# A two-layer DiT block on one core: maxima over partitions by a TensorE product in the FFN and the w_out stage

## The chip, the core and the metric

The kernel runs on one core of a Trainium2 chip. Its time is the device time of one execution in microseconds. Three runs of the kernel before took 3187.04, 3192.05 and 3198.25 us, median 3192.05. One more execution was profiled; it took 3185.58 us.

## The reference

Two layers over 1024 tokens (`x`) and 256 context tokens (`ctx`), width 1024. The context is carried only through layer 0. Everything is float32.

```python
for l in range(2):
    mod, mod_c = silu(c) @ w_ada[l] + b_ada[l], silu(c_ctx) @ w_ada[l] + b_ada[l]   # shifts, scales, gates
    h = modulate(layer_norm(x), sh1, sc1)              # the same for ctx
    qa, ka, va, qb, kb, vb, zh, zf = split(h @ w_in[l])
    oa = banded_window_attention(rope(qa), rope(ka), va, ctx keys and values, sink)
    ob = blockwise_full_attention(rope(rms(qb)), rope(rms(kb)), vb, ctx keys and values)
    oc = hyena_mixer(zh); od = fnet_mixer(zf)          # long convolution, Fourier mixing
    y = rms_per_group(oa, ob, oc, od) * g @ w_out[l] + b_out[l]
    x = layer_norm(4 ** 0.25 * x + g1 * y)
    h2 = modulate(layer_norm(x), sh2, sc2)
    a, g = split(dwconv3(h2 @ w_up + b_up))            # 2 x 2752 columns, convolution over tokens
    x = layer_norm(4 ** 0.25 * x + g2 * ((silu(a) * g) @ w_down + b_down))
```

## The kernel before

**Products in pairs of float16.** Nearly every float32 operand of a product is scaled by a power of two and split into two float16 parts, `hi` and `lo`; a product is then three matmuls (hi*hi, hi*lo, lo*hi). The power of two (`pow2`, L79) comes from a bound on the whole operand, so the kernel often needs the largest absolute value of a tile over its free dimension and over its 128 partitions. VectorE's reduction gives the first. The second is `allmax` (L89): for each column of its input two copies of 64 partitions, a maximum, four copies of 32 partitions, a maximum broadcast to 32 columns, a 32x32 block transpose and a reduction, ten VectorE instructions, in the tiles `arc` and `arb` of a pool with one buffer.

**Weights.** `load_w` (L375) fetches a weight tile of float32 into `wraw` (four buffers, 512 KB each, shared by all weight loads and the residuals), reduces it on VectorE, calls `most` (L109) and so `allmax`, and splits it with ScalarE (hi) and VectorE (lo) into `w16` tiles (four buffers). w_in and w_out are bounded by the root of a sum of squares instead (`root`, L119), which calls `allmax` too. `load_wd` (L1263) does the same for up to three 128-row tiles of w_down at once.

**Stages of a layer.** `project` (products with w_in, beside hyena and FNet work), `attend`, `out_proj` (w_out, residual, two normalizations, the FFN's input `h2` in float16 pairs) and `ffn`. In `out_proj` three up tiles are loaded ahead (`UA`, L985 to L987).

**The FFN** (L1027). The 5504 up columns are 43 tiles of 128: one tile of 64 + 64 columns (`w_upl`, column 42), worked first as a group of its own, and 21 pairs (gate half and value half) in seven groups of three. `up` (L1058) takes a weight tile that was loaded ahead or loads it, multiplies it with all tokens (48 matmuls of 512 columns, in layer 0 another 24 of 256 for the context) into the PSUM tile `ux` (two buffers in layer 0, three in layer 1), and applies bias and convolution on ScalarE (L1077) and VectorE (L1078, L1080) with a correction of the two edge tokens on GpSimd. A pair is multiplied after SiLU and reduced to its maximum (L1168). At the end of a group `load_wd` brings w_down's rows, `allmax` turns the group's maxima into one scale (`gm`, `gsp`), `gh` and `gl` are split, and `down` and `add` multiply them with w_down into `dps` (PSUM, two buffers) and add to `acc` on VectorE (L1112). The first half of the tokens is added right away, the second half after the next group's scale, so that these matmuls lie beside that chain.

**The last group** has the residual and the gate worked into `acc` beside it (`residual`, L1119), and its sums go tile by tile through the final normalization (`first`, `second`); in layer 0 a third `dps` buffer comes in here (`fdx`, L1144), and `third` builds the next layer's input. In layer 0 the FFN also carries layer 1's hyena filter (`filter_ahead`, L1323), whose PSUM tile `fps` has a pool of one bank.

**Order of the work.** The code is traced in program order; a planner then orders each engine's instructions before the run, by readiness in its own time model and by program order among what is ready. On the chip each engine follows the written order and waits on semaphores. Buffers of one tile name are handed out by the planner as earlier ones come free.

Of the kernel before, what the change touches and what calls it, by code (L numbers as in the profile page):

```python
# [59 lines left out]
class Kernel:  # L60
# [28 lines left out]
    def allmax(self, out, in_):  # L89


        v = self.nc.vector
        for i in range(in_.shape[1]):
            x = in_[:, i:i + 1]
            c = self.ar.tile([128, 4], FT, name="arc")
            for h in (0, 64):
                v.tensor_copy(c[h:h + 64, 0:1], x[64 - h:128 - h])
            v.tensor_tensor(c[:, 1:2], x, c[:, 0:1], op=OP.max)
            for q in range(0, 128, 32):
                v.tensor_copy(c[q:q + 32, 2:3], c[q ^ 32:(q ^ 32) + 32, 1:2])  # L100
            b = self.ar.tile([128, 2, 32], FT, name="arb")
            v.tensor_tensor(b[:, 0], c[:, 1:2].to_broadcast([128, 32]), c[:, 2:3].to_broadcast([128, 32]), op=OP.max)
            v.transpose(b[:, 1], b[:, 0])
            v.tensor_reduce(out[:, i:i + 1], b[:, 1], axis=AX.X, op=OP.max)
# [38 lines left out]
    def consts(self):  # L143
# [5 lines left out]
        nc.vector.tensor_copy(self.identh, self.identf)  # L149
        self.mhalf = p.tile([128, 8], FT, name="mhalf")  # L150
# [15 lines left out]
    def tables(self):  # L166
# [9 lines left out]
        nc.vector.tensor_scalar(self.mask, mk, -(2.0 ** 50), None, op0=OP.mult)  # L176
        self.bigi = p.tile([128, 128], BF, name="bigi")
        nc.vector.tensor_scalar(self.bigi, self.identf, 2.0 ** 50, None, op0=OP.mult)
# [157 lines left out]
    def start(self):  # L336
# [3 lines left out]
        self.bgp = self.pool("bgp", self.p2, bufs=3, space=PSUM, side=self.sides[1])  # L340
        with ExitStack() as es:
# [66 lines left out]
    def run(self, out):  # L408
        for l in range(2):
            self.l = l  # L410
            self.p2 = ExitStack()
            if l == 0:
                self.start()
            else:
                self.bgp = self.pool("bgp", self.p2, bufs=3, space=PSUM, side=self.sides[1])
            self.project(l)
# [262 lines left out]
    def attend(self, l):  # L679
        nc = self.nc  # L680
        A, B = self.sides
        with ExitStack() as es:
            tp = self.pool("atm", es, bufs=2, side=A)
            pt = self.pool("atp", es, space=PSUM, side=A)
            po = self.pool("ato", es, space=PSUM, side=B)
            nt = NT if l == 0 else NX
# [18 lines left out]
    def att_main(self, l, tp, pt, pq):  # L705
# [29 lines left out]
        def top(ch, h):  # L735
# [9 lines left out]
            for t in range(nq):  # L745
# [7 lines left out]
                for i, (k0, k1) in enumerate(parts):  # L753
# [6 lines left out]
                    for b, m in masks:  # L760
                        nc.tensor.matmul(ps[:, (b - k0) * 128:(b - k0 + 1) * 128], self.bigi, self.mask[:, m],
# [33 lines left out]
        def scores(ch, h, b0, i, k, q0, q1):  # L795
# [12 lines left out]
            for b, m in masks:  # L808
                nc.tensor.matmul(ps[:, (b - b0) * 128:(b - b0 + 1) * 128], self.bigi, self.mask[:, m],
                                 start=False, stop=True, skip_group_check=True)  # L810
# [148 lines left out]
    def out_proj(self, l):  # L959
# [6 lines left out]
        with ExitStack() as es:  # L966
# [6 lines left out]
            pp = self.pool("oph", es, bufs=2, space=PSUM, side=B)  # L973
            lg, lb = self.row_bcast(cp, a["ln1_g"][l], "rlg"), self.row_bcast(cp, a["ln1_b"][l], "rlb")
# [52 lines left out]
    def ffn(self, l, out):  # L1027
# [6 lines left out]
        with ExitStack() as es:  # L1034
# [10 lines left out]
            dp = self.pool("fdp", es, bufs=2, space=PSUM, side=B)  # L1045
            eup = es.enter_context(ExitStack())
# [11 lines left out]
            def up(col, src, pool, early=False):  # L1058

                whi, wlo, winv = self.upw.pop(0) if self.upw else self.load_w(src, 128, None, sp, "up")  # L1060
# [3 lines left out]
                parts = [(pp.tile([128, 1024], FT, name="ux", bufs=2 + l), 0, L)]  # L1064
# [71 lines left out]
            if l == 0:  # L1136
                self.bg = [self.filter_ahead(1, self.pool("fha", eha, side=B), self.pool("fpp", eha, space=PSUM, side=B))]
            for gi, grp in enumerate(groups):
                if gi == len(groups) - 1:
# [3 lines left out]
                    if l == 0:  # L1143
                        dpr.append(self.pool("fdx", es, bufs=1, space=PSUM, side=B))  # L1144
# [6 lines left out]
                for i, j in enumerate(grp):  # L1151
                    k = 128
                    if j < 21:
                        g32 = up(2 * j, a["w_up"][l, j, :, :, 0:128], g3)
                        if gi == len(groups) - 1:
                            self.tick(RT[0])
                        ug = up(2 * j + 1, a["w_up"][l, j, :, :, 128:256], tp)
                        nc.scalar.activation(g32, g32, AF.Silu)
                        nc.vector.tensor_mul(g32, g32, ug)
                    else:  # L1160
                        k = 64
                        g32 = up(42, a["w_upl"][l], g3, True)
# [780 lines left out]
```

## Time and profile before

| | |
|---|---|
| profiled execution | 3185.58 us |
| its span, first to last instruction | 3183.8 us |
| TensorE matmuls (PE) | 2849.6 us busy, 90% |
| TensorE weight loads (PEld) | 1510.6 us, 47% |
| VectorE (DVE) | 2474.5 us, 78% |
| ScalarE (ACT) | 1315.0 us, 41% |
| GpSimd (POOL) | 864.4 us, 27% |
| mean granted TensorE clock | 0.946 of full speed |
| chain that ended last | TensorE 52%, VectorE 32% of the span |

In the profile the FFN of layer 0 runs from about 860 to 1740 us and that of layer 1 from about 2420 us to the end; `out_proj` lies ahead of each. An instruction's row gives its line in the kernel, its engine, operation, output and input tiles. A value in brackets, with an arrow, is time that the engine stood idle just before, and the instruction that ended the wait. In a row of a group of instructions, the figures after the bar are busy time, mean length of one in ns, and idle time before them with what ended most of it. A matmul's length holds its passage through the array; in a stream they start closer together than they are long.

### The profile page before, as it was taken

The numbers are of one execution on the slowest core, as the hardware profiler recorded it, in microseconds if no ns is written. First come the engines' busy times: TensorE is split into PE (matmuls) and PEld (weight loads), VectorE is DVE, ScalarE is ACT, GpSimd is POOL, SyncE is SP. The second block draws the span as 40 slices with busy tenths as digits, with TensorE's granted clock in tenths as the row PEclk, the third lists the DMA queues.
The fourth block names the chain that finished last, engine by engine and source line by source line (L and its number), as shares of the span: only waits on it lengthen the run. The fifth ranks groups of instructions, "written<-read, shape, count | busy, mean of one in ns | idle before, by whom it ended". The sixth has DMA issues, their size and how long they took to land.

```text
span 3183.8 us, 46231 instructions
## 1 busy us (share of the span) xinstructions
PE 2849.6 (90%) x17268; PEld 1510.6 (47%) x17268; DVE 2474.5 (78%) x5678; ACT 1315.0 (41%) x2098; POOL 864.4 (27%) x886
## 2 busy tenths in 40 slices
PE   5998878899999999999999799967898799999997
PEld 1567744345444554544544356734554244444443
DVE  4989578865788677677588789789976878777788
ACT  3566555554543222222223765665655222222222
POOL 1337335643500000000020736446633000000022
PEclk8999979999999999999999899967999899999998
DMA  7253465561311121121120344442022122111121
GB/s 260 84 174 105 137 208 186 174 206 67 125 44 55 37 67 50 34 67 50 34 94 33 119 146 128 145 130 61 22 79 76 53 60 60 37 50 40 54 86 53
DMA packets 214926, 293.76 MB, mean 92 GB/s; under 512 B 36189, under 2 KB 156425, under 8 KB 213549
## 3 DMA queue, kind: packets, MB, share of 16 engines
q1 hardware_dynamic: 205629, 269.57, 26.4%
q0 software_dynamic: 9072, 21.24, 2.5%
q8 instruction: 135, 2.21, 0.3%
q14 instruction: 90, 0.74, 0.1%
HBM read 240.05 MB, written 50.71 MB: 91 GB/s over the span
## 4 chain that ended last, share of the span: by engine, by line
PE 52%; DVE 32%; DMA 5%; ACT 4%; issue 4%; POOL 3%; SPq 0%; DVEq 0%; POOLq 0%; ACTq 0%
PE ux L1073 24%; PE uc L1073 3%; DVE M L763 2%; DVE acc L1112 2%; PE ada L216 2%; PE dps L1092 2%; PE zps L562 2%; PE zps L563 2%; PE zps L561 2%; DVE ph L816 2%; PE dps L1094 2%; PE dps L1095 2%; DVE arc L100 2%; DVE gl L140 2%; DMA wraw<-in_w_up 1%
## 5 line engine op out<-in xcount | busy, mean ns | idle before, releaser
L1073 PE MATMUL ux<-h2h,w 128*128 128x512 f16 x2752 | 836.0, 381 | 11.2 <-ACT w L139 4.8
L1073 PEld LDWEIGHTS <-w 128*128 128x128 f16 x5160 | 503.6, 98 | 523.4 <-issue 13.1
L1073 PE MATMUL ux<-h2l,w 128*128 128x512 f16 x1376 | 523.6, 381 | 0.6 <-POOL h2l L325 0.6
L1083 POOL TENSOR_TENSOR u<-u,ed 128x2 f32<-128x2 f32 x129 | 34.0, 263 | 1331.9 <-DVE u L1080 1208.5
L1092 PE MATMUL dps<-wdh,gh 128*128 128x512 f16 x792 | 307.7, 389 | 71.1 <-DVE acc L1112 24.3
L817 POOL TENSOR_TENSOR pl<-p,ph 128x512 f16<-128x512 f32 (+1 forms) x224 | 239.5, 1084 | 195.6 <-DVE ph L816 115.0
L1094 PE MATMUL dps<-wdl,gh 128*128 128x512 f16 x756 | 291.4, 385 | 0.0
L1095 PE MATMUL dps<-wdh,gl 128*128 128x512 f16 x756 | 289.8, 384 | 0.0
L1078 DVE SCALAR_TENSOR_TENSOR u<-ux,ws,u 128x1023 f32<-128x1023 f32 x86 | 109.7, 1278 | 228.9 <-ACT u L1077 228.8
L1077 ACT ACTIVATE u<-ux,cb,ws 128x1024 f32<-128x1024 f32 x86 | 103.2, 1202 | 415.5 <-PE ux L1073 415.0
L812 ACT ACTIVATE p<-sps,al 128x512 f32<-128x512 f32 (+3 forms) x288 | 169.7, 618 | 121.9 <-PE sps L806 41.5
L763 DVE TENSOR_REDUCE M<-mps 128x1 f32<-128x512 f32 (+2 forms) x336 | 173.3, 535 | 31.9 <-PE mps L758 18.5
L139 ACT ACTIVATE w<-wraw,upp 128x1024 f16<-128x1024 f32 x80 | 91.6, 1144 | 223.0 <-DVE upp L86 223.0
L758 PE MATMUL mps<-kT,qT 128*128 128x512 f16 (+2 forms) x336 | 116.7, 365 | 61.9 <-DVE M L763 58.4
L561 PE MATMUL zps<-w,hh 128*128 128x256 f16 x608 | 168.1, 276 | 2.4 <-ACT zt L608 2.4
L563 PE MATMUL zps<-w,hl 128*128 128x256 f16 x608 | 168.5, 277 | 0.0
L562 PE MATMUL zps<-w,hh 128*128 128x256 f16 x608 | 168.5, 277 | 0.0
L1112 DVE SCALAR_TENSOR_TENSOR acc<-dps,gm,acc 128x512 f32<-128x512 f32 x198 | 146.6, 743 | 6.7 <-PE dps L1095 5.5
L1092 PEld LDWEIGHTS <-gh 128*128 128x128 f16 x792 | 78.4, 99 | 133.1 <-DVE gh L140 21.8
L139 ACT ACTIVATE gh<-u,gsp 128x640 f16<-128x640 f32 (+3 forms) x88 | 61.5, 764 | 190.9 <-DVE gsp L86 175.2
L1094 PEld LDWEIGHTS <-gh 128*128 128x128 f16 x756 | 74.8, 99 | 130.3 <-issue 52.0
L816 DVE CAST ph<-p 128x512 f16<-128x512 f32 (+3 forms) x200 | 115.3, 587 | 26.8 <-ACT p L812 25.6
(562 smaller groups left out, 6878.2 us busy)
## 6 DMA issues: line engine op xcount, KB each, us to landing
wraw<-in_w_ada SPq DMA_DIRECT2D x96, 512.0 KB
wraw<-in_w_up SPq DMA_DIRECT2D x84, 512.0 KB
wraw<-in_w_down SPq DMA_DIRECT2D x42, 512.0 KB
wraw<-in_w_in SPq DMA_DIRECT2D x32, 512.0 KB
wraw<-xd SPq DMA_DIRECT2D x26, 512.0 KB
xd<-rx SPq DMA_DIRECT2D x18, 512.0 KB
wraw<-in_w_out SPq DMA_DIRECT2D x16, 512.0 KB
M<-in_k_mf POOLq DMA_DIRECT2D x24, 256.0 KB, 3.6
```

Of the source, the lines that this page charges most:

```text
L561: nc.tensor.matmul(ps, ah[:, kt], bh[:, kt], start=kt == ks[0], stop=False)
L562: nc.tensor.matmul(ps, ah[:, kt], bl[:, kt], start=False, stop=False)
L563: nc.tensor.matmul(ps, al[:, kt], bh[:, kt], start=False, stop=kt == ks[-1])
L763: nc.vector.tensor_reduce(M[:, t, i:i + 1], ps[:, :n], axis=AX.X, op=OP.max)
L812: nc.scalar.activation(p32, ps[:, c], AF.Exp, scale=self.al[ch][:, 0:1])
L816: nc.vector.tensor_copy(ph[:, c], p32)
L817: (nc.vector if i % 4 == 2 else nc.gpsimd).tensor_tensor(pl[:, c], p32, ph[:, c], op=OP.subtract)
L1073: nc.tensor.matmul(o, w[:, kt], h[:, kt, t0:t0 + n], start=first, stop=last)
L1092: nc.tensor.matmul(ps, gh[:, i, c], w[0][:, i, hc], start=f, stop=False)
L1094: nc.tensor.matmul(ps, gh[:, i, c], w[1][:, i, hc], start=False, stop=False)
L1095: nc.tensor.matmul(ps, gl[:, i, c], w[0][:, i, hc], start=False, stop=e)
L1112: nc.vector.scalar_tensor_tensor(acc[t][:, hc], ps, sc, bt[:, hc] if gi == 0 else acc[t][:, hc], op0=OP.mult, op1=OP.add)
```

## The change

`allmax` gets a second form, used where `self.mx` gives a PSUM tile: for each column the upper 16 bits of the float32 maxima (a bfloat16 with the same exponent) are the stationary operand, broadcast to 128 columns, and the identity is the moving operand. Each of the 128 output partitions then holds all 128 maxima, and one VectorE reduction gives the largest. `self.mx` is set in `out_proj` and `ffn`; at the start, in `project` and in `attend` the ten copies stay, under the name `allmax_copies`.

For its PSUM tile `out_proj` opens a bank of its own (`opm`). In `ffn` the pool `fpp` serves both the maxima and the filter's tiles, in both layers; `ux` has two buffers in layer 1 as well, and the third `dps` buffer of layer 0's last group goes.

`up` no longer loads its own tile. At each call, if fewer than three tiles are waiting, the next of the list is loaded; then the oldest is taken, so that a load stands two tiles ahead of its use in program order. In attention the mask's factor 2^100 sits in the mask alone, and the identity in bfloat16 takes the place of `bigi`.

```diff
     def allmax(self, out, in_):
+        if self.mx is None:
+            return self.allmax_copies(out, in_)
+        nc = self.nc
+        n = in_.shape[1]
+        ps = self.mx()[:, :n * 128].rearrange("p (n q) -> p n q", n=n)
+        for c in range(n):
+            m = in_[:, c:c + 1].bitcast(BF)[:, 1:2]
+            nc.tensor.matmul(ps[:, c], m.to_broadcast([128, 128]), self.identb, start=True, stop=True)
+        nc.vector.tensor_reduce(out, ps, axis=AX.X, op=OP.max)
+
+    def allmax_copies(self, out, in_):
...
+        self.identb = p.tile([128, 128], BF, name="identb")
+        nc.vector.tensor_copy(self.identb, self.identf)
...
-        nc.vector.tensor_scalar(self.mask, mk, -(2.0 ** 50), None, op0=OP.mult)
-        self.bigi = p.tile([128, 128], BF, name="bigi")
-        nc.vector.tensor_scalar(self.bigi, self.identf, 2.0 ** 50, None, op0=OP.mult)
+        nc.vector.tensor_scalar(self.mask, mk, -(2.0 ** 100), None, op0=OP.mult)
...
             pp = self.pool("oph", es, bufs=2, space=PSUM, side=B)
+            mp = self.pool("opm", es, bufs=1, space=PSUM, side=B)
+            self.mx = lambda: mp.tile([128, 512], FT, name="mx")
...
             dp = self.pool("fdp", es, bufs=2, space=PSUM, side=B)
+            mp = self.pool("fpp", es, space=PSUM, side=B)
+            self.mx = lambda: mp.tile([128, 512], FT, name="fps")
...
-            def up(col, src, pool, early=False):
-                whi, wlo, winv = self.upw.pop(0) if self.upw else self.load_w(src, 128, None, sp, "up")
+            srcs = [a["w_upl"][l]] + [a["w_up"][l, j, :, :, i * 128:(i + 1) * 128] for j in range(21) for i in range(2)]
+            srcs = srcs[len(self.upw):]
+            def up(col, pool, early=False):
+                if srcs and len(self.upw) < 3:
+                    self.upw.append(self.load_w(srcs.pop(0), 128, None, sp, "up"))
+                whi, wlo, winv = self.upw.pop(0)
...
-                parts = [(pp.tile([128, 1024], FT, name="ux", bufs=2 + l), 0, L)]
+                parts = [(pp.tile([128, 1024], FT, name="ux", bufs=2), 0, L)]
...
-                self.bg = [self.filter_ahead(1, self.pool("fha", eha, side=B), self.pool("fpp", eha, space=PSUM, side=B))]
+                self.bg = [self.filter_ahead(1, self.pool("fha", eha, side=B), mp)]
...
-                    if l == 0:
-                        dpr.append(self.pool("fdx", es, bufs=1, space=PSUM, side=B))
```

## Rows read from the trace of the kernel before

**Rows 1.** Windows: length; busy (count) of PE, PEld, DVE, ACT, POOL; clock; DMA; GB/s.

```profile
860.00:1000.00 140.00, 124.97 (x608) 58.98 (x606) 116.04 (x278) 59.49 (x77) 13.01 (x27) 0.91 0.16 48
1000.00:1600.00 600.00, 589.31 (x3054) 299.14 (x3053) 427.80 (x979) 140.81 (x147) 23.90 (x63) 1.00 0.16 49
1600.00:1800.00 200.00, 173.17 (x834) 83.66 (x833) 164.97 (x399) 77.14 (x101) 65.89 (x65) 0.94 0.24 80
2420.00:2580.00 160.00, 122.86 (x532) 52.49 (x531) 125.11 (x323) 50.98 (x56) 13.65 (x20) 0.88 0.18 54
2580.00:3000.00 420.00, 414.06 (x1908) 186.06 (x1906) 321.69 (x747) 106.18 (x105) 8.92 (x28) 1.00 0.17 52
3000.00:3184.00 184.00, 154.65 (x702) 68.71 (x700) 153.11 (x302) 48.48 (x55) 46.38 (x36) 0.94 0.17 60
2540.00:2560.00 20.00, 12.49 (x47) 4.86 (x47) 18.88 (x78) 5.97 (x8) 0.00 (x0) 0.72 0.17 52
```

**Rows 2.** TensorE's timeline, layer 1's entry: start, length, instruction [idle before, releaser].

```profile
2481.67 0.61 PE L1092 MATMUL dps<-wdh,gh 128*128 128x512 f16 x1 [20.80 <-DVE gh L140]
2547.12 0.61 PE L1092 MATMUL dps<-wdh,gh 128*128 128x512 f16 x1 [6.32 <-ACT gh L139]
```

**Rows 3.** VectorE's timeline over the same stretch.

```profile
2423.66 2.33 DVE L395 TENSOR_REDUCE upmx<-wraw 128x1 f32<-128x1024 f32 x2
2474.00 0.31 DVE L97 COPY arc<-gm 64x1 f32<-64x1 f32 x2
2477.92 0.31 DVE L97 COPY arc<-upmx 64x1 f32<-64x1 f32 x2
```

**Rows 4.** Copies' groups: busy us, mean ns, idle before.

```profile
L97 DVE COPY arc<-upmx 64x1 f32<-64x1 f32 x160 | 23.7, 148 | 3.7
L98 DVE TENSOR_TENSOR arc<-upmx,arc 128x1 f32<-128x1 f32 x80 | 13.5, 169 | 0.0
L100 DVE COPY arc<-arc 32x1 f32<-32x1 f32 x600 | 87.0, 145 | 11.7
L102 DVE TENSOR_TENSOR arb<-arc 128x32 f32<-128x32 f32 x150 | 34.0, 227 | 1.1
L103 DVE STREAM_TRANSPOSE arb<-arb 128x32 f32<-128x32 f32 x150 | 30.8, 205 | 1.7
L104 DVE TENSOR_REDUCE upmo<-arb 128x1 f32<-128x32 f32 x80 | 14.5, 181 | 1.0
```

**Rows 5.** Groups by shape: score reductions, mask product, up weight loads.

```profile
L763 DVE TENSOR_REDUCE M<-mps 128x1 f32<-128x256 f32 x160 | 65.4, 415 | 11.4 <-PE mps L758 10.5 <-PE mps L761 0.2
L763 DVE TENSOR_REDUCE M<-mps 128x1 f32<-128x512 f32 x128 | 85.5, 681 | 9.7 <-PE mps L758 8.0 <-PE po L829 0.9
L809 PE MATMUL sps<-mask,bigi 128*128 128x128 bf16 x112 | 19.5, 221 | 0.0
L1073 PEld LDWEIGHTS <-w 128*128 128x128 f16 x5160 | 503.6, 98 | 523.4 <-issue 13.1 <-ACT w L139 7.7 <-DVE w L140 6.2
```

**Rows 6.** TensorE's timeline in attention: two mask products in a row.

```profile
653.82 0.28 PE L809 MATMUL sps<-mask,bigi 128*128 128x128 bf16 x2
```

**Rows 7.** TensorE's groups: up matmuls and score products, with what they waited for.

```profile
L1073 PE MATMUL ux<-h2h,w 128*128 128x512 f16 x2752 | 836.0, 381 | 11.2 <-ACT w L139 4.8 <-DVE upp L84 2.6 <-DVE w L140 1.5
L758 PE MATMUL mps<-kT,qT 128*128 128x512 f16 (+2 forms) x336 | 116.7, 365 | 61.9 <-DVE M L763 58.4 <-DMA kT<-kT 2.5
```

**Rows 8.** Idle time before the reductions L395, then L1276: us, times.

```profile
  DMA wraw<-in_w_up: 36.5, 35
...
  DMA wraw<-in_w_down: 27.6, 19
```

**Rows 9.** TensorE's waits, 2580 to 3000: us, times, longest.

```profile
PE dps L1092 <- DVE acc L1112: 2.9, 4, 0.7
PE ux L1073 <- ACT w L139: 2.6, 4, 0.6
```

**Rows 10.** Who waited for the gated add into acc: us, times.

```profile
  PE dps L1092: 14.6, 9
```

More of the change, by code (lines that the diff above doesn't have):

```diff
@@ L340, in start @@
         self.bgp = self.pool("bgp", self.p2, bufs=3, space=PSUM, side=self.sides[1])
+        self.mx = None
         with ExitStack() as es:
@@ L415, in run @@
                 self.bgp = self.pool("bgp", self.p2, bufs=3, space=PSUM, side=self.sides[1])
+                self.mx = None
             self.project(l)
@@ L685, in attend @@
             po = self.pool("ato", es, space=PSUM, side=B)
+            self.mx = None
             nt = NT if l == 0 else NX
@@ L760, in top @@
                     for b, m in masks:
-                        nc.tensor.matmul(ps[:, (b - k0) * 128:(b - k0 + 1) * 128], self.bigi, self.mask[:, m],
+                        nc.tensor.matmul(ps[:, (b - k0) * 128:(b - k0 + 1) * 128], self.identb, self.mask[:, m],
                                          start=False, stop=True, skip_group_check=True)
@@ L808, in scores @@
             for b, m in masks:
-                nc.tensor.matmul(ps[:, (b - b0) * 128:(b - b0 + 1) * 128], self.bigi, self.mask[:, m],
+                nc.tensor.matmul(ps[:, (b - b0) * 128:(b - b0 + 1) * 128], self.identb, self.mask[:, m],
                                  start=False, stop=True, skip_group_check=True)
@@ L1153, in ffn @@
                     if j < 21:
-                        g32 = up(2 * j, a["w_up"][l, j, :, :, 0:128], g3)
+                        g32 = up(2 * j, g3)
                         if gi == len(groups) - 1:
                             self.tick(RT[0])
-                        ug = up(2 * j + 1, a["w_up"][l, j, :, :, 128:256], tp)
+                        ug = up(2 * j + 1, tp)
                         nc.scalar.activation(g32, g32, AF.Silu)
@@ L1161, in ffn @@
                         k = 64
-                        g32 = up(42, a["w_upl"][l], g3, True)
+                        g32 = up(42, g3, True)
                         ug = tp.tile([128, nn], FT, name="u")
```

## The prediction

> **What bounds the kernel now.** I read the busy times by stage first, then TensorE's two longest stands in one of them, then VectorE's order there. By stage [rows 1], TensorE is the bound in both FFN stages: in the middle of them it is busy 589.3 of 600 us (layer 0) and 414.1 of 420 us (layer 1), at a granted clock of 1.00, the full 2.4 GHz. VectorE is busy 428 of 600 and 322 of 420 us there. So VectorE time taken away in the middle is worth nothing by itself; what can be won is the time in which TensorE stands or runs slowly: 15.0 us in 860 to 1000 (clock 0.91), 26.8 in 1600 to 1800, 37.1 in 2420 to 2580 (clock 0.88), and 10.7 and 5.9 us in the two middles. The end, 3000 to 3184, has 29.4 us, most of it the last normalization, after TensorE's last product.
>
> TensorE's own timeline names what ends the two longest stands at layer 1's entry [rows 2]: 20.8 us until the `gh` of the first group (only w_up's last 128 columns) is there, and 6.3 us until the next group's. VectorE's order beside them [rows 3] gives the cause: at 2423.66 it has already reduced two up tiles, but the first copy of an up tile's maximum (L97, `arc<-upmx`) comes at 2477.92, behind those of `gm` at 2474.00. `arc` has one buffer, given out in program order, and `gm` needs the group's last FFN tile. So weights that have long landed wait for the group to end, and TensorE has neither `gh` nor weights.
>
> **The change part by part.**
>
> 1. *Maxima over partitions.* One by copies is 2 x 148 (L97) + 169 (L98) + 4 x 145 (L100) + 227 + 205 + 181 ns = 1.66 us in ten VectorE instructions [rows 4]. Of 150 (count of L102), 23 keep the copies (16 for w_in, 4 for w_out, 2 for the gains, 1 first bound); 127 go through TensorE, by 121 reductions, because three calls carry three columns each. The reduction of 128x128 from PSUM is not in the trace: 256 columns take 415 ns and 512 take 681 [rows 5], 1.04 ns a column, so 0.28 us by this line (0.18, the 32-column L104, to 0.415 from below and above). VectorE: -127 x 1.66 + 118 x 0.28 + 3 x 0.55 = -176 us, nearly all of it beside TensorE's work. It counts only at the ends of stages, below.
>
> 2. *Products on TensorE.* A 128x128 bf16 product is there, as the mask product: 221 ns alone [rows 5], but two in 0.28 us [rows 6], so 0.06 us a piece in a stream; a weight load, as those of L1073, is 98 ns [rows 5]. I take 0.10 us, the load, since a 0.06 us product does not cover the next one: 127 x 0.10 = +13 us (ends 0.06 and 0.27: 8 and 34).
>
> 3. *Waits at these products.* The planner writes TensorE's order down before the run; a product whose maximum is late holds all matmuls behind it, and the FFN waits for those. Nearest by place and kind is the up matmul's wait for its weights, 4.8 + 2.6 + 1.5 us = 8.9 us [rows 7], over 86 tiles 0.10 us each; the attention's score products, as tightly coupled to VectorE, wait 58.4 us in 336, 0.17 each [rows 7]. I take 0.10: +13 us. Ends: 0 (each in the shadow of a running matmul) and 0.28, 36 us, if about a quarter of VectorE's mean wait for a transfer, 1.0 to 1.5 us [rows 8], is handed on at every product.
>
> 4. *Up weights two tiles ahead.* The first two tiles of the next group now stand in program order ahead of the group's `gm`. Their maxima no longer queue behind it, and the 6.3 us stand at 2547 [rows 2] and its slow stretch (clock 0.72 in 2540 to 2560 [rows 1]) have matmuls to fill them. At the first stand (20.8 us) the next tile to load is still behind `gm`, since three wait already and the first group loads none; but the chain from `gm` to the weights falls from ten queued copies to a product and a reduction: I reckon 5 us earlier. Layer 1's entry: 5 + 6 + about 3 for the smaller waits + 6 for slow matmuls = -20 us (ends -5 and -45 of the 37 us idle and up to 0.12 x 160 = 19 us of clock). Layer 0's entry, the same pattern with 15 us idle and up to 0.09 x 140 = 13 of clock: -10 (0 to -20). The middles: 16.6 us idle; in layer 1's, 2.6 of 5.9 us is the wait for a group's first up weights [rows 9], which I expect to go, and I take a share somewhat smaller of both: -6 (0 to -14).
>
> 5. *Last groups.* There residuals and normalizations load VectorE (153 of 184 us, 165 of 200 [rows 1]). About eight maxima less by copies are 8 x (1.66 - 0.28) = 11 us of VectorE in a last group, and layer 1's h vectors three more in 1720 to 1800. I take half of it for each: -5 in layer 1 and -7 in layer 0 (0 to -8, 0 to -15).
>
> 6. *PSUM.* Layer 1's up tiles go from three to two buffers. In the middle I cost that at nothing: layer 0 has two already, and TensorE is busy 589.3 of 600 us there [rows 1]. At layer 1's entry the third tile's first half can't run early; it moves into the 20.8 us stand, which the 5 us above already assume. In layer 0's last group the third `dps` buffer goes: TensorE already waits 14.6 us in nine waits for the second add into `acc` [rows 10]. I take +4 (0 to +12). The filter's tiles and the maxima now share one bank in layer 0: I take 0, since a `gm` that waits for a filter tile has the `dps` matmuls of the group before and two loaded up tiles as cover; without it each of six groups would stand as at 2547, 6 x 6.3 = 38 us, which the range holds. The masks' factor moves from one operand to the other: 0, same instructions.
>
> Sum: -20 - 10 - 6 - 5 - 7 + 13 + 13 + 4 = -18 us. The profiled execution was 3185.58 us (its span of 3183.8 and 1.8 us around it): 3167.6. It lies 6.5 us under the median of the three timed runs, so the forecast for a median is 3174.
>
> What is late next at the entries: the group's own `gm` chain through the up result's two adds, and then VectorE's `acc` adds.
>
> **A rule against it.** In the middle of layer 1 TensorE waits some 0.65 us at a time, eight times, and the granted clock stays 1.00 [rows 1, 9]. The Trainium skill, "TensorE: Matmul & The Clock Gate", section "A second HAM failure mode: psum-queue depth-cycling", tells of a kernel in which many short idle times between groups of matmuls drove the clock back and forth between its levels. The row speaks against it for waits of this size; the sum without it stands at 3174. If it held, every group boundary would look like 2540 to 2560, where at most 0.28 x 20 = 5.6 us are lost [rows 1]: 14 boundaries, +78, 3252 us.
>
> **The rivals.**
>
> - *TensorE stands at the products (slower).* Place: each of the 127 products, above all those of up and down weights, whose reductions on VectorE wait for transfers: 36.5 us in 35 waits and 27.6 in 19, 1.0 and 1.5 us a time [rows 8]. Today that falls into VectorE's slack. The price is the mean stand s: 127 x s. It decides from s = (48 - 13 - 4)/127 = 0.24 us on; at 0.5, half of such a wait at every product, 3185.6 - 48 + 13 + 4 + 64 + 6.5 = 3225. For it: the order is fixed, and waits are counted in rows. Against it: the up reductions of 2423.66 were done some 50 us before their maxima were taken [rows 3], so only some products would wait. The Trainium skill, the same page, Part 3, section "The mechanism", says that matmuls start and end strictly in order; no row here shows one that overtakes another.
> - *The entries keep their idle time (no change).* Two `ux` buffers and the third up tile behind `gm` leave layer 1's entry as it is: -5 instead of -20, sum -3, 3189.
> - *Nearly all idle time goes.* If the shorter chains fill both entries, the middles and the ends to the ends given (-45, -20, -14, -8, -15), with 8 for products and 12 for waits, the sum is -82: 3110. Against it: the waits for `acc` stay, and they are 2.9 of the 5.5 us that TensorE waits in layer 1's middle [rows 9].
> - *The clock rule above*: 3252; the rows bear it out poorly.
> - *That the change does not do what it says* I give no share of its own: which calls take the product is plain in the code.
>
> **How the numbers follow.** Chances: forecast (3140 to 3182) 0.44; nearly all idle time gone 0.10; no change 0.18; products stand 0.25; clock 0.03. About 0.3%, 10 us, is what a measurement of this kernel can tell from no change. Faster 0.54, same 0.18, slower 0.28. The range that holds it 8 times in 10: from 3120 (half of the third case left out) to 3228 (the first rival up to s = 0.5). The signs are mixed, so the likeliest case's own range stands above.
>
> **What would show it.** VectorE's busy time falls by about 176 us, L97 to L103 counts to 23 maxima, TensorE has 127 more products. Right: the stand before `dps` at layer 1's entry is under 10 us and that at its second group gone; the middle groups of layer 1 stay within 1.5 us of the present pace. Wrong: idle time before the new products over 30 us in sum, middle groups longer by over 2 us each, or a clock under 1.00 in the middles.

## The result and the profile after

The changed kernel takes 3146.1 us (median of four runs, 3145.4 to 3150.9) against 3195.2 for the kernel before on the same chip: ratio 0.9857, 95% interval [0.984, 0.9874]. Forecast were 3174 us; the sign is right, the time is in the range, and the gain, 49 us instead of 18, is 2.7 times the forecast. The profiled execution took 3150.9 us (span 3149.1), the slowest of the four.

By stage, as [rows 1], but for the last window, which ends with the span:

```profile
860.00:1000.00 140.00, 130.66 (x678) 66.07 (x679) 97.04 (x174) 55.48 (x69) 21.57 (x33) 0.96 0.17 53
1000.00:1600.00 600.00, 597.87 (x3130) 302.87 (x3129) 396.19 (x655) 154.53 (x170) 18.02 (x62) 1.00 0.18 53
1600.00:1800.00 200.00, 171.26 (x853) 84.69 (x851) 160.03 (x302) 85.85 (x115) 72.99 (x73) 0.96 0.23 79
2420.00:2580.00 160.00, 146.31 (x651) 64.49 (x650) 119.58 (x208) 54.28 (x57) 13.32 (x22) 0.94 0.19 58
2540.00:2560.00 20.00, 20.00 (x96) 8.82 (x94) 16.82 (x37) 8.45 (x10) 0.39 (x2) 1.00 0.17 53
2580.00:3000.00 420.00, 420.00 (x1975) 191.58 (x1973) 294.65 (x470) 106.33 (x108) 16.46 (x29) 1.00 0.18 52
3000.00:3149.00 149.00, 121.92 (x558) 54.19 (x556) 120.82 (x186) 40.56 (x47) 37.36 (x32) 0.93 0.19 67
```

The reader is to see TensorE's first number. In layer 1's middle it is busy 420.00 of 420 us (414.06 before), in layer 0's 597.87 of 600 (589.31). At layer 1's entry it is busy 146.31 of 160 (122.86) at a clock of 0.94 (0.88), and 2540 to 2560, the second group's stand, is full. The last groups have not gained: 149 us with 27 idle, as 184 with 29.

TensorE's timeline at layer 1's entry, its three longest waits from 2440 on, to set beside [rows 2] (ahead of them it waits 1.86 and 4.27 us for `oxn`, out of which `h2` is made; before, 2.41):

```profile
2455.78 0.61 PE L1098 MATMUL ux<-h2h,w 128*128 128x512 f16 x1 [4.57 <-DVE u L1105]
2472.85 0.38 PE L1117 MATMUL dps<-wdh,gh 128*128 128x512 f16 x1 [1.32 <-DVE upp L84]
2476.34 1.03 PE L1098 MATMUL ux<-h2h,w 128*128 128x512 f16 x2 [0.95 <-DVE w L153]
```

The 20.80 us before the first `dps` are gone (it starts at 2468.41 without a wait, and a later one waits 1.32), the second group's 6.32 are gone, and a wait for a `ux` buffer (4.57 us) is new. The first of these is the doing of the two `ux` buffers: the third up tile's matmuls, which the kernel before ran ahead of the stand, now begin at 2455.78 and fill it (x5_psum below has this change alone, and loses that stand too). The weights still queue behind `gm` at this place. Four more up tiles have been reduced by 2435.40, but their products come only behind `gm`'s, and both take the tile `fps` now, as both took `arc` before (VectorE's timeline, then TensorE's):

```profile
2434.18 1.22 DVE L409 TENSOR_REDUCE upmx<-wraw 128x1 f32<-128x1024 f32 x1 [1.61 <-DMA wraw<-in_w_up]
```

```profile
2464.42 0.22 PE L99 MATMUL fps<-identb,gm 128*128 128x128 bf16 x1
2468.36 0.22 PE L99 MATMUL fps<-identb,upmx 128*128 128x128 bf16 x1
```

VectorE's groups, with TensorE's group of the new product last (mean ns of one behind the comma, then idle before them):

```profile
L100 DVE TENSOR_REDUCE upmo<-fps 128x1 f32<-128x128 f32 x80 | 22.7, 284 | 52.7 <-PE fps L99 52.7
L115 DVE TENSOR_TENSOR arb<-arc 128x32 f32<-128x32 f32 x23 | 9.6, 419 | 0.2
L99 PE MATMUL fps<-identb,upmx 128*128 128x128 bf16 x80 | 17.7, 222 | 0.8 <-DVE upmx L409 0.8
```

23 maxima keep the copies, a reduction is 0.284 us (forecast 0.28), and TensorE idles 0.8 us in all for these products by this view. VectorE idles 52.7 us in front of these reductions, which costs nothing in layer 1's middle, where TensorE is busy throughout.

### The profile page after: what moved, and what is told of

The parts are those of the page before. It is cut to its first block, busy times and chain, and to the rows that moved or that the text cites. A ratio compares the mean times of both kernels' runs of the same rounds, so it can differ in the third digit from the quotient of the medians.

```text
span 3149.1 us, 45348 instructions
## 1 busy us (share of the span) xinstructions
PE 2863.9 (91%) x17395; PEld 1524.8 (48%) x17395; DVE 2332.7 (74%) x4529; ACT 1313.3 (42%) x2098; POOL 854.5 (27%) x886
## 4 chain that ended last, share of the span: by engine, by line
PE 54%; DVE 27%; DMA 7%; ACT 5%; issue 4%; POOL 3%; SPq 0%; DVEq 0%; POOLq 0%; ACTq 0%
PE ux L1098 22%; PE dps L1117 4%; PE dps L1119 3%; PE dps L1120 3%; DMA wraw<-in_w_up 3%; DVE M L779 2%; DVE ph L832 2%; PE ada L229 2%; PE uc L1098 2%; PE zps L577 2%; PE zps L576 2%; PE zps L578 2%; DVE w L153 1%; DVE pl L833 1%; PE bg L1590 1%
## 5 line engine op out<-in xcount | busy, mean ns | idle before, releaser
L409 DVE TENSOR_REDUCE upmx<-wraw 128x1 f32<-128x1024 f32 x80 | 97.3, 1217 | 107.4 <-DMA wraw<-in_w_up 107.2
L843 PE MATMUL po<-vh,ph 128*128 128x65 f16 x976 | 124.2, 200 | 8.2 <-DVE ph L832 3.7
```

## The experiments

All runs stand in one table. Each time is a median beside the kernel before on the same chip. The stages are worked out from TensorE's starts in each run's one profiled execution: *FFN 0* from layer 0's first `ux` to its last `dps`, *FFN 1* from layer 1's first `ux` to the end, *entry 1* and *middle 1* the parts of FFN 1 to column 13 and from there to column 37 (up tiles in the order of the work, counted from 0: 13 opens the third group of three pairs, 37 the last), *outside* all else. In x18 and the runs with tiles ahead entry 1 holds fewer down products than in the kernel before (in the changed kernel by 15.5 us, worked out in the section on the prediction).

```
run             us      ratio to before          FFN 0   FFN 1  entry 1  middle 1  outside
before          -       -                        968.3   763.3  231.0    387.6     1452.2
changed kernel  3146.1  0.9857 [0.984, 0.9874]   945.6   731.8  190.8    374.7     1471.7
x15_again       3142.2  0.9866 [0.9843, 0.989]   946.1   733.6  193.1    374.7     1460.7
x1_consts       3199.1  1.0025 [1.0015, 1.0034]  965.2   763.1  230.5    387.7     1468.8
x2_ahead        3169.6  0.9921 [0.9904, 0.9938]  956.8   741.9  200.2    381.5     1462.9
x3_product      3318.6  1.0401 [1.0385, 1.0417]  1046.6  806.5  233.8    415.4     1463.0
x4_arc4         3245.0  1.0166 [1.0152, 1.018]   978.1   784.8  235.2    393.5     1479.5
x5_psum         3205.1  1.0038 [1.0026, 1.0051]  971.1   762.7  221.3    391.7     1461.2
x6_twice        3154.4  0.9879 [0.9866, 0.9892]  953.7   737.0  194.0    376.5     1460.7
x7_aheadcopies  3177.2  0.9947 [0.9935, 0.9959]  960.7   741.4  197.6    380.9     1473.5
x8_one          3170.5  0.9937 [0.9924, 0.9949]  958.7   749.3  201.7    379.8     1460.3
x9_three        3145.7  0.986 [0.9841, 0.9878]   942.8   732.3  189.1    374.7     1466.1
x10_dps3        3147.5  0.9866 [0.9849, 0.9884]  945.8   738.8  193.3    374.7     1457.5
x11_late        3148.3  0.9866 [0.9851, 0.9881]  953.8   733.9  192.9    374.7     1454.7
x12_gmcopies    3130.6  0.981 [0.9797, 0.9824]   946.2   728.5  187.9    374.5     1453.5
x13_gmonly      3145.7  0.9855 [0.9842, 0.9869]  943.9   731.2  190.7    377.3     1470.3
x16_ffnonly     3152.0  0.9884 [0.987, 0.9898]   945.5   726.8  186.5    374.5     1477.2
x17_twoarcs     3164.1  0.9907 [0.9892, 0.9922]  946.2   736.9  191.3    382.2     1474.1
x18_beforearcs  3159.9  0.989 [0.9877, 0.9904]   942.6   745.0  190.0    373.6     1469.4
x19_gmthree     3138.7  0.983 [0.9816, 0.9844]   944.5   728.4  187.4    374.5     1470.7
```

**The same kernel again (x15_again, no edit).** 

> The changed kernel unchanged, a second profiled execution and more times. It tells how far one execution's time ahead of the first FFN is chance: up to 12.5 us by the same instructions (585.9 and 573.4 us at the first instruction whose order differs). Expected 3145 to 3147, with ux first in layer 0 at 858 to 866 instead of 874.2. If it is at 870 or more again, that part belongs to the kernel.

The second execution, in the same order of instructions on every engine, has 862.9 us ahead of the first FFN where the first had 874.2, and the FFNs within 2 us of it. By this one pair the FFN columns can be compared to some 2 us, the last column only to some 11; both FFNs together are the measure below: 1731.6 us before, 1677.4 and 1679.7 after.

**Two tiles ahead alone (x2_ahead).**

```diff
+                if srcs and len(self.upw) < 3:
+                    self.upw.append(self.load_w(srcs.pop(0), 128, None, sp, "up"))
```

> Up weights two tiles ahead, maxima by copies everywhere, PSUM as before. Queue theory: the first two tiles of each group pass the group's maximum; the stand at layer 1's second group and the slow stretch there go, the first stand at its entry stays about 20 us: 3160 to 3175. VectorE theory: the same copies are made, so within 8 us of 3195. Order theory: anything within 15 us.

Both FFNs take 1698.7 us, as the first theory has it: 33 of the 54 us come from this alone. The second group's stand is gone, the first group's is not (TensorE's timeline):

```profile
2480.75 0.61 PE L1097 MATMUL dps<-wdh,gh 128*128 128x512 f16 x1 [20.81 <-DVE gh L140]
```

**The product alone (x3_product):** the changed kernel with each up tile loaded at its own turn.

```diff
-                if srcs and len(self.upw) < 3:
-                    self.upw.append(self.load_w(srcs.pop(0), 128, None, sp, "up"))
-                whi, wlo, winv = self.upw.pop(0)
+                whi, wlo, winv = self.upw.pop(0) if self.upw else self.load_w(src, 128, None, sp, "up")
```

> Maxima by the TensorE product in the FFN and the w_out stage with its PSUM layout, but each up tile loaded at its own turn as before. Queue theory: the queue behind the group's maximum is still there but each link is shorter, so about half of the gain: 3165 to 3180, with the stand at layer 1's second group still over 2 us. VectorE theory: nearly the whole gain, 3145 to 3155, since VectorE loses the same 142 us.

4.0% slower, which neither theory had. The waits over the whole run (us, times, longest), then TensorE's timeline at one group of layer 0:

```profile
PE fps L99 <- DVE gm L1192: 47.0, 12, 7.1
PE fps L99 <- DVE upmo L100: 12.1, 9, 5.1
```

```profile
1132.99 0.29 PE L99 MATMUL fps<-identb,gm 128*128 128x128 bf16 x1 [6.89 <-DVE gm L1192]
1133.66 0.27 PE L99 MATMUL fps<-identb,upmx 128*128 128x128 bf16 x1 [0.38 <-DVE gm L100]
1134.31 0.27 PE L99 MATMUL fps<-identb,upmx 128*128 128x128 bf16 x1 [0.38 <-DVE upmo L100]
```

TensorE stands 6.89 us at the product of `gm`, and the weights' products come only behind it. This is the prediction's first rival, and it is real where no loaded up tile lies ahead in TensorE's order. Behind such a stand the granted clock falls as well: 0.51 in 1130 to 1140, and 0.95 in 1000 to 1600, where the changed kernel has 1.00:

```profile
1130.00:1140.00 10.00, 5.86 (x17) 2.02 (x18) 9.48 (x27) 5.64 (x8) 0.00 (x0) 0.51 0.00 1
1000.00:1600.00 600.00, 549.55 (x2781) 273.30 (x2782) 340.69 (x569) 132.84 (x148) 9.89 (x51) 0.95 0.15 45
```

So the price is more than the stands themselves: TensorE's idle time in both FFNs rises by 73 us, their length by 121.5. The Trainium skill, "TensorE: Matmul & The Clock Gate", Part 3, section "The mechanism", says that matmuls start and end strictly in order; these 12 waits agree.

**One tile ahead (x8_one), three (x9_three).**

```diff
-                if srcs and len(self.upw) < 3:
+                if srcs and len(self.upw) < 2:    # x9_three: < 4
```

> The changed kernel with one up tile loaded ahead instead of two. If one tile is enough to cover the product of gm (its wait is one chain of VectorE and ScalarE behind the last up tile, some 7 us a time in the run without any tile ahead, against 10 to 13 us of matmuls that one tile holds in the layers): 3146 to 3160, the middles as now. If the weights' own chain (maximum, scale, two splits) needs a second tile of time: stands come back at gm's product and at ux, half of the 126 us or so: 3190 to 3230.

> The changed kernel with three up tiles loaded ahead instead of two. By the theory that a maximum can't pass an earlier one in the program's order, the third up tile of the next group now passes the group's gm as well, so that layer 1's entry loses what is left of its stand: 5 to 10 us at layer 1's entry (dps first and column 7 earlier by that much), little elsewhere: 3136 to 3142. Rival: what ends the entry is the ux buffer and the group's own chain, and a fourth set of weights only takes buffers away: 3146 or more.

One tile takes most of the stands away, neither as little nor as much as expected: the FFNs take 1708.0 us, 28 to 31 more than with two; entry 1 is 9 to 11 us longer, middle 1 5. Three tiles take 2 to 5 us more from the FFNs (1675.1) and nothing measurable from the whole.

**More buffers for the copies (x4_arc4).**

```diff
-        self.ar = self.pool("ar", bufs=1)
+        self.ar = self.pool("ar", bufs=4)
```

(The masks' staging tile moved into a shared buffer for room.)

> The kernel before with four buffers for the copies' tiles arc and arb instead of one (the raw mask goes through a weight buffer at the start to make room). Queue theory: up tiles whose reductions are done no longer wait for the group's maximum; both stands at layer 1's entry shrink (20.8 us to under 12, 6.3 us to under 2): 3155 to 3175. VectorE theory: the same work on VectorE, within 8 us of 3195. Order theory: anything within 15 us.

Slower by 1.7%, which no theory had, and why it is slower is not shown. VectorE's timeline at layer 1's entry: the reductions of the up tiles, and the first copies of `gm` and of up tiles.

```profile
2460.65 2.33 DVE L395 TENSOR_REDUCE upmx<-wraw 128x1 f32<-128x1024 f32 x2
2511.08 0.31 DVE L97 COPY arc<-gm 64x1 f32<-64x1 f32 x2
2511.42 0.99 DVE L97 COPY arc<-upmx 64x1 f32<-64x1 f32 x6
```

With four buffers the up tiles' copies still wait for `gm`'s, 50 us behind their reductions, and then come all at once. So it is not the number of buffers, four for one, that holds them back.

**A list of its own for `gm` (x18_beforearcs).** The kernel before, whose only other edit is that the masks' staging tile is freed early:

```diff
-            c = self.ar.tile([128, 4], FT, name="arc")
+            c = self.ar.tile([128, 4], FT, name="arc" + tag)
-            b = self.ar.tile([128, 2, 32], FT, name="arb")
+            b = self.ar.tile([128, 2, 32], FT, name="arb" + tag)
-                self.allmax(m1[:, 1:2], m1[:, 0:1])
+                self.allmax(m1[:, 1:2], m1[:, 0:1], "g")
```

> The kernel before with gm's copies in tiles of their own name, nothing else but the masks' staging tile. This is my prediction's cause by itself (weights that have landed wait for gm's tile). If the list alone held the next group's weights back, layer 1's entry falls from 231 us towards 200 and both FFNs from 1732 to about 1700: 3155 to 3170. If it is that the planner writes the next group's loads down behind gm anyway, so that the copies come in the same order: 1728 to 1734, 3188 to 3200.

This is the decisive run for the prediction's cause: 0.989 [0.9877, 0.9904], both FFNs 1687.6 us, with no product and no load moved ahead. VectorE's timeline at layer 1's entry:

```profile
2415.16 2.33 DVE L397 TENSOR_REDUCE upmx<-wraw 128x1 f32<-128x1024 f32 x2
2421.84 0.31 DVE L97 COPY arc<-upmx 64x1 f32<-64x1 f32 x2
2427.72 0.31 DVE L97 COPY arc<-upmx 64x1 f32<-64x1 f32 x2
2474.44 0.31 DVE L97 COPY arcg<-gm 64x1 f32<-64x1 f32 x2
```

The up tiles' copies now come 4 us behind the end of their reductions and 53 us ahead of `gm`'s; in [rows 3] they came behind it. With x4 this says: the planner hands out tiles of one name in program order, with four buffers as with one; a second name lets the weights pass. VectorE's work is that of before (432 us in 1000 to 1600, 428 before), and TensorE's idle time there is gone all the same (596.8 busy of 600). What this version lacks beside the changed kernel shows in its last group, in TensorE's waits from 2600 on:

```profile
PE dps L1094 <- DVE acc L1119: 13.5, 3, 12.0
```

**Copies everywhere: one list (x7_aheadcopies), two (x17_twoarcs).** The changed kernel without products; in x17 with the names of x18.

```diff
-        if self.mx is None:
+        if True:
             return self.allmax_copies(out, in_)
```

> The changed kernel with every maximum still by copies: two tiles ahead, the PSUM layout of the changed kernel (one bank reserved and not used), the changed masks. Beside the run with two tiles ahead alone (3170) it tells what the PSUM layout costs, beside the changed kernel (3146) what the product is worth on top. Theory that the product is worth some 24 us once weights lie ahead, PSUM nothing: 3170 within 6. Theory that giving up the buffers costs and the product gives back more: 3177 to 3190, stands of the third up tile for ux and of dps for acc in the last groups.

> Two up tiles ahead and the changed PSUM layout with every maximum by copies, as in an earlier run (3177; both FFNs 1702 us), but gm's copies in two small tiles of their own name, so that gm and the weights no longer wait for each other in one list. The masks' staging tile is freed early for the room. Theory of the shared list: both FFNs take 1675 to 1683 us, layer 1's entry (first ux to column 13) 188 to 191 instead of 197.6: total 3145 to 3158. Theory of the shorter chain and VectorE's load: the FFNs stay at 1698 to 1704, total 3170 to 3182.

The FFNs take 1702.1 and 1683.1 us, 1677.4 and 1679.7 with the products: two lists without products are worth 19 us, where the products bring 22 to 25 on top of the tiles ahead. x7's FFNs are 3 us longer than x2's, so the changed PSUM layout costs little there. In total x17 gains less than expected (3164), because of the time outside the FFNs (1474.1). In layer 1's middle x7 still shows waits (2632 to 3013: its window, then its wait for the adds):

```profile
2632.00:3013.00 381.00, 374.85 (x1730) 169.04 (x1728) 294.14 (x708) 95.29 (x96) 8.14 (x24) 1.00 0.17 50
```

```profile
PE dps L1117 <- DVE acc L1137: 4.2, 8, 1.2
```

and x17 has 382.2 us there, 374.7 with products. I took these waits for the adds into `acc` for a matter of VectorE's load. x18 says no, in the same stretch, with as many copies and 0.5 us of such waits:

```profile
2588.00:2962.00 374.00, 373.52 (x1731) 169.22 (x1730) 295.52 (x687) 94.78 (x97) 6.14 (x24) 1.00 0.18 53
```

They hang on the planner's order; which part of it (tiles ahead, two `ux` buffers) makes them in x17 and not in x18 is open. The row of x7 also shows the granted clock at 1.00 beside eight waits of up to 1.2 us; in x3, with stands of up to 7.1 us, it fell. The Trainium skill, "TensorE: Matmul & The Clock Gate", section "A second HAM failure mode: psum-queue depth-cycling", tells of a kernel whose clock went back and forth at frequent short idle times between groups of matmuls; for waits of x7's size the trace does not agree.

**Half of the products (x12_gmcopies, x13_gmonly, x16_ffnonly).** In the changed kernel, `gm` by copies (16 maxima by the trace; the expectation counted 14); or `gm` and the h vectors by products and all weights by copies; or x12 with copies also in `out_proj` (12 maxima by the trace, of the h vectors and the up tiles loaded there; the expectation counted eight) and its PSUM bank left out.

```diff
-                self.allmax(m1[:, 1:2], m1[:, 0:1])      # x12_gmcopies, x16_ffnonly
+                self.allmax_copies(m1[:, 1:2], m1[:, 0:1])
-        self.allmax(m[:, 1:2], mx)                       # x13_gmonly, in most()
+        self.allmax_copies(m[:, 1:2], mx)
-            self.mx = lambda: mp.tile([128, 512], FT, name="mx")   # x16_ffnonly
```

> The changed kernel with the 14 maxima of gm alone by copies again, those of the weights and of the h vectors by products. Theory that the product pays at the entries through the short chain behind gm: layer 1's first dps later by about 8 us and layer 0's entry by some 4 to 8, the middles as in the changed kernel: 3154 to 3162. Rival, that it pays through VectorE's load in the middles and the last groups: 14 maxima are little of it, 3146 to 3150.

> The other half: the changed kernel with the maxima of the up, down and w_out weights by copies and those of gm and the h vectors by products. Theory of VectorE's load: the adds into acc come late again, four groups in the middle of layer 1 take 381 us as with copies everywhere (374.7 in the changed kernel), and the last groups lose some 10 us each: 3162 to 3172. Rival, that the entries' gm chain is what pays: 3146 to 3152.

> The version with gm by copies, and the eight maxima of out_proj's stages (w_out, h vectors, up weights loaded there) by copies as well: products only for weights in the FFNs. Theory that TensorE's idle time in the FFNs is used up by either half of the products and that the 15 us between that version and the changed kernel come from the order ahead of the FFNs: 3128 to 3140, the FFN stages as there. Theory that out_proj's products pay: 3138 to 3150, later by some 8 us between the first ops and the first ux.

x12 and x16 missed both of their theories, x13 its first. Either half gives the whole gain in the FFNs: 1674.7 with the weights' products, 1675.1 with those of `gm` and the h vectors. Either takes `gm` and the weights out of one list, as x18 does: in x12 the first up tile's maximum is taken 40 us ahead of `gm`'s (TensorE's timeline, then VectorE's).

```profile
2409.55 0.22 PE L99 MATMUL fps<-identb,upmx 128*128 128x128 bf16 x1
```

```profile
2449.26 0.31 DVE L110 COPY arc<-gm 64x1 f32<-64x1 f32 x2
```

The changed kernel gets as far with one list, each user of which holds it for a shorter time. The stage's middle is then TensorE's, with next to nothing left for the other half (374.5 us in x12, 377.3 in x13, 374.7 in the changed kernel):

```profile
2588.00:2962.00 374.00, 374.00 (x1755) 170.52 (x1754) 263.98 (x457) 93.98 (x97) 8.30 (x24) 1.00 0.18 51
```

(x12, layer 1's middle: TensorE is busy 374.00 of 374 us.) In x12 and x13 the first `dps` of layer 1 comes 57.8 and 67.3 us after the first `ux`, 51.1 in the changed kernel, and yet the entries are not longer: TensorE has up tiles to multiply. How early `gh` is there does not decide, how much other work lies in front of it does.

x12 is the fastest version, 11 to 16 us below the changed kernel (by two timings, each also taken beside the kernel before on its chip) and 0.981 [0.9797, 0.9824] of before. 3 to 5 us of that lie in the FFNs; the rest is outside, where x16, whose FFNs are still shorter (1672.3), has 1477.2 us and 3152. Of these 24 us between x12 and x16 only 3 lie between the first `ops` and the first `ux`, where the expectation looked; 21 lie ahead of it. There the two orders part at 571 us, where x16's copies for the h vectors come in beside the attention. Why that costs as much is open.

**x12 with three tiles ahead (x19_gmthree):** the edits of both. 

> The fastest version so far (gm's maxima by copies, all others in these stages by products: 3131) with three up tiles ahead. Three tiles took 5 us from layer 0's entry and 2 to 4 from layer 1's in the changed kernel, hidden in its order outside the FFNs: FFNs 1668 to 1673 us against 1674.7, total 3124 to 3131 if the order outside stays, up to 3150 if it moves as in other runs (outside 1453 to 1477).

The FFNs take 1672.9 us, as expected; outside moves by more than that, and 3139 is no gain over x12.

**What the products cost (x6_twice).**

```diff
-            nc.tensor.matmul(ps[:, c], m.to_broadcast([128, 128]), self.identb, start=True, stop=True)
+            for _ in range(2):
+                nc.tensor.matmul(ps[:, c], m.to_broadcast([128, 128]), self.identb, start=True, stop=True)
```

> The changed kernel with each of the 127 products over partitions made twice into the same columns. It measures what one product more costs. Cheap-product theory (my step 2, corrected by the trace after: 0.056 us start to start in a stream): 127 x 0.056 = 7 us, at my forecast's price of 0.10 us 13 us: 3153 to 3159 over the changed kernel's 3146; only the planner's order, which moves with the longer step, may add or take some 10 us. Rival, TensorE stands at the products and every ns there is handed on to VectorE's chain and back: over 20 us, 3166 or more.

+8.4 us over the first timing of the changed kernel, as expected, 8.4/127 = 0.066 us each (+12 over the second, 0.10; the scatter does not tell these apart). In the trace one follows another start in the stream by 0.056 us.

**The PSUM given up (x5_psum), the constants (x1_consts), the identity written later (x11_late), a third dps buffer (x10_dps3).**

```diff
-                parts = [(pp.tile([128, 1024], FT, name="ux", bufs=2 + l), 0, L)]    # x5_psum, fdx left out too
+                parts = [(pp.tile([128, 1024], FT, name="ux", bufs=2), 0, L)]
+        self.identb = p.tile([128, 128], BF, name="identb")          # x1_consts; x11_late: in tables()
-            dp = self.pool("fdp", es, bufs=2, space=PSUM, side=B)    # x10_dps3
+            dp = self.pool("fdp", es, bufs=2 + l, space=PSUM, side=B)
```

> The kernel before with two of the three ux buffers in layer 1 and without the third dps buffer of layer 0's last group: the PSUM that the change gives up, alone. My step 6: 0 for ux and +4 for the dps buffer, 3196. Rival: the third ux buffer did work at layer 1's entry and its last group, where the changed kernel waits 4.57 us for one: +10 or more, 3202 to 3210, the shift seen in layer 1.

> The kernel before with the mask factor moved and the bf16 identity added, nothing else. Queue theory (the gain comes from weights that no longer stand behind a group's maximum): no change outside the planner's shifts, 3195 us within 10 us. Theory of VectorE time (the gain comes from the 142 us of VectorE work taken away): the same, 3195. Theory of the planner's order (one more instruction at the start reorders the early stages and most of the gain is luck of the order): a change of 15 us or more to either side.

> The changed kernel with the bf16 identity written where the kernel before wrote its scaled one (beside the masks, by the same kind of instruction), instead of among the first instructions. Theory that the constants cost 6.6 us by moving the planner's order from 77 us on: the order ahead of the first FFN is that of before again, ux first in layer 0 near 860 to 864, 3137 to 3142. Rival: what differs ahead of the FFNs is from one execution to the next only: 3143 to 3149.

> The changed kernel with a third dps buffer in layer 1, in the bank that the third ux buffer gave up. Theory that what is left at layer 1's entry and in its last group is TensorE's wait for the adds into acc: -2 to -6, 3140 to 3144, in the last group. Rival: what is late is the up result (u, 4.6 us) and the last normalization, no dps buffer: 3146 within 3.

TensorE's timeline in x5 at layer 1's entry: the third up tile, the first `dps`, and the second group's.

```profile
2472.80 0.61 PE L1073 MATMUL ux<-h2h,w 128*128 128x512 f16 x1 [4.57 <-DVE u L1080]
2485.89 0.38 PE L1092 MATMUL dps<-wdh,gh 128*128 128x512 f16 x1
2550.21 0.61 PE L1092 MATMUL dps<-wdh,gh 128*128 128x512 f16 x1 [7.77 <-ACT gh L139]
```

The 20.80 us before the first `dps` are gone with the third `ux` buffer alone, down to the same wait of 4.57 us that the changed kernel has; the second group's stand needs the tiles ahead (x2). x5 in sum: slower by 0.38%, the size of its rival and not for its reason: only 2 us of it lie in the FFNs (1733.8), entry 1 is 10 us shorter, not longer, middle and last group are 9 longer, and layer 0's last group loses 2 (226.9 for 224.7 from column 37 to the last `dps`). x1: 0.25% slower, nothing of it in the FFNs; the order differs from 77 us on. x11, which restores that early order, has 1454.7 us outside, but FFN 0 is 8 us longer, and the whole is no faster than the changed kernel; the runs do not show why. x10: no gain; it lengthens FFN 1 by 5 to 7 us.

## Why the prediction was half right

The entries' and last groups' lengths have to be set right first: at column 13 the changed kernel has done 63 (layer 0) and 72 (layer 1) down products fewer than the kernel before, and does them in the last groups. At 0.2155 us from start to start that is 13.6 and 15.5 us, moved and not won. In layer 0 another 4.9 us of the filter's matmuls moved from the entry to the middle. By equal work, with the cost of the new products in every figure:

- **Step 4, the failed one.** Entries: -10 and -20 forecast, -12 and -25 measured (255.6 to 225.1, 231.0 to 190.8, less the moved work). Middles: -6 forecast, -21 measured (488.0 to 485.1, 387.6 to 374.7, and the moved filter). The cause was named half right: "`arc` has one buffer, given out in program order". The program order of one list is the cause (x18: -44 us in the FFNs with two names), the one buffer is not (x4). The change does not take the list apart, as x18 does: it puts two tiles ahead of `gm` in it (x2: -33) and holds it for a shorter time (the products on top: -22 to -25; whether by the shorter hold alone or by VectorE's freed time too, no run separates). I priced the parts of the stands that I saw and not what this gives in every group: idle time between TensorE's instructions falls in entry 1 from 38.0 to 13.7 us, in middle 1 from 9.6 to 0.0. "The waits for `acc` stay" is wrong: in layer 1's middle they are gone in the changed kernel, and 0.5 us is left of them in x18.
- **Steps 2 and 3**, +13 and +13, were too dear: 127 x 0.056 = 7 us, and the distance from a product's start to the next matmul's, with the stands, is 0.113 us in the mean, so another 127 x 0.057 = 7 us. Step 3 asked how often a product would be late and not what lies in front of it. With nothing ahead it costs 126 us and is the first rival; with two tiles ahead next to nothing. The two edits are not a sum: -23 alone, +126 alone, -49 together.
- **Step 5**: -5 (layer 1) and -7 (layer 0) forecast, +6 and -3 measured. The new place of the down products is not what costs layer 1 its 6 us: x2 has them there too and its last group takes as long as before by equal work (160.2 less 15.5, for 144.7 from column 37 to the end). x5 loses 5 us there with the PSUM given up alone.
- **Step 6**: +4 forecast, with nothing for the third `ux` buffer; by x5 +2 in the FFNs and +12 in all. But that buffer is not worth nothing at layer 1's entry: without it the entry is 10 us shorter, because its third tile's matmuls fill the stand. The step saw them move there and took the 5 us of step 4 to hold it.
- **Step 1**: -176 us of VectorE forecast, 2474.5 - 2332.7 = 142 measured. Its instructions' lengths add up to 167.5 us less (2790.6 to 2623.1), but some lie in each other's time, and busy time counts that once. It had no part in the sum.
- **Not foreseen**: the order outside the FFNs. The FFNs gain 52 to 54 us, the whole 49; x1 has +6.6 for it.

The signs asked for came: no stand before the first `dps` and 1.32 us before a later one, the second group's gone, 127 more products. The first of them is luck for the argument: x5 has it without the products and without tiles ahead. Layer 1's middle groups are 3.2 us shorter, against "within 1.5 us". Of the rivals, "nearly all idle time goes" describes layer 1's middle, "products stand" the version without tiles ahead; "the entries keep their idle time" and the clock rule fall for the changed kernel; in x3 the clock does fall.

## What to carry to other kernels

Where loaded data waits beside an idle engine, look which small scratch tiles it shares with the slow chain: tiles of one name went out in program order here, with four buffers as with one, and a second name for one user won most of what the new algorithm did (44 of 52 to 54 us in the FFNs). Where work moves into an engine that runs in order, ask first what independent work stands in front of it. Once TensorE is full in a stage, a second cure there brings nothing, so try each half alone.

## What was not expected of the hardware

One program, executed twice in the same order on every engine, differed by 11.3 us in its first 870 us and by less than 2 us in each FFN. Nearly all of the 11 us comes up between 100 and 135 us, and the granted clock goes with it: it stays at the lower of its levels in one execution and not in the other (changed kernel, then x15, 100 to 120). Just ahead of it, in 80 to 100, TensorE was busy 16.93 and 17.47 of 20 us, at 0.78 and 0.67.

```profile
100.00:120.00 20.00, 20.00 (x51) 9.93 (x49) 8.24 (x17) 3.68 (x5) 3.19 (x3) 0.50 0.15 49
100.00:120.00 20.00, 17.84 (x74) 8.95 (x73) 14.67 (x30) 6.83 (x12) 6.03 (x6) 0.90 0.15 53
```

The same stages of layer 1, from layer 0's last `dps` to layer 1's first `ops`, took 506.0 and 506.1 us. So the kind of work does not explain the scatter; why the clock rose later in one execution is open.

A 128x128 bf16 product with its own weight load of 98 ns takes 0.056 us from start to start in a stream: the load did not set the pace, which step 2 had assumed.
